# One weight cast of the recurrence tied behind the last turned block, gate differences in three steps, and first value products ahead of second transposes

## The chip, the core and the metric

The kernel runs on one NeuronCore of one Trainium2 chip. The core has a matrix engine (TensorE, written PE; its weight loads are written PEld), a vector engine (VectorE, DVE), an activation engine (ScalarE, ACT), a general engine (GpSimd, POOL) and a queue that issues most transfers (SyncE, SP). Each engine works through its own queue of instructions in the order in which the program was built; a wait on another engine's work stands in that queue too, and what is queued behind a waiting instruction waits with it. The metric is device time in microseconds, the median of several runs.

## The reference, cut to what matters

A hybrid block on 1024 tokens of width 1024, in float32: stick-breaking attention (8 heads of 64) and a gated linear recurrence (HGRN2, 4 heads of 128) on the same normalised input, merged by gates, then a squared-ReLU MLP and a final norm.

```
xn = rmsnorm(x, norm1_g)
u = xn @ w_in            # q, k, v | f, i, q, g of the recurrence | two gates
o_sb = stick_breaking_attention(q_sb, k_sb, v_sb)       # masked, cumulative in log space
k_hg = (1 - lb) * sigmoid(-f_raw)
o_hg = hgrn2_chunkwise(silu(q_hg), k_hg, i_hg, log_f)   # state carried over chunks
o_hg = rmsnorm(o_hg, hg_norm_g) * silu(g_hg)
merged = sigmoid(gate_sb + b) * (o_sb @ w_o_sb) + sigmoid(gate_hg + b) * (o_hg @ w_o_hg)
h = x + merged @ w_out
h = h + square(relu(rmsnorm(h, norm2_g) @ w_ff1)) @ w_ff2
return rmsnorm(h, final_g)
```

## The kernel before, in words

Every float32 operand of a product is split into a high part (cast to fp32r on ACT, `hi_copy`, line 156) and a low part (the difference, on DVE, `lo_sub`, line 161), and a product is three matrix products: high by high, high by low, low by high (`three`). So each weight matrix is loaded by SP, cast on ACT, subtracted on DVE, and then used by PE.

Work goes out in two lanes. The main lane is attention, then the recurrence. The fill lane, a `Stream` of jobs, is a list of projections (query and key of a head, the recurrence's f, q and i, the gates) whose bodies yield after a few products; `st.advance(n, upto)` lets n such steps out between two steps of the main lane. When a job starts, `prefetch` splits the weights of the next job and loads those of the one after. A builder then orders each engine's instructions from these two lanes and from the dependencies; `after(a, b)` adds the plain rule that a is not ordered ahead of b on its engine, with no semaphore.

Three places of this order matter here.

- The start. Tokens are normalised two blocks of 128 at a time (x0 and x1, then x2 and x3). `norm_transpose` turns a pair of blocks on PE into eight PSUM tiles xnt (one of 128 columns by 256 tokens for each of the eight parts of the width); ACT writes the high part xnh from each, DVE the low part xnl, and then the PSUM bank is free again. The fill job of this stage has the products for query and key of head 0 (pjqk, 24 of them for a pair of blocks) and for the values (pjv; with the high part wvh of the weight first, then with the low part wvl).
- The gate units (`RawUnit`, names wga0 to wga9; wga8 and wga9 belong to the output gates of the recurrence and stand inside the attention stage). Besides the split of its first half such a unit needs a difference of two weight pieces (`sub`, 128x1024), then a difference of the two halves of that (`sub`, 128x512), and the split of the result (names wga8t, wga9t: a cast on ACT and a subtraction on DVE). `Stream.step` calls `split_t` for the unit of the next job at the sixth step of the job in front of it, with all three at once.
- The end of attention. Each block of attention is turned on PE (pw), split into wTh on ACT and wTl on DVE (`turn`), and used by the value products po. The weight of the recurrence's input, `u_i`, has four pieces wir0 to wir3, which share two load buffers with other weights; its first piece is cast (wih0) when `hg_levels(0)` begins, with no rule on where that cast stands among the casts of the last turned blocks. In the recurrence's first step DVE and ACT make the pairs sd, which PE sums (sd products with ones).

Of the kernel before, what the change touches and what calls it, by code (L numbers as in the profile page):

```python
# [39 lines left out]
def kernel(  # L40
# [34 lines left out]
    def slot(name, dt=F32):  # L75
        return spool.tile([P, 1024], dt, tag="s", name=name)
# [28 lines left out]
    def after(ins, earlier):  # L105
        if earlier is not None and earlier.ins is not ins.ins:
            tc.add_manual_dep(ins.ins, earlier.ins.name, NOSYNC, reason="issue order")
        return ins
# [55 lines left out]
    def hi_lo(h, l, src):  # L164
        hi_copy(h, src)
        return lo_sub(l, src, h)
# [266 lines left out]
    class Unit:  # L433
# [5 lines left out]
        def split_t(self):  # L439
            pass  # L440
# [46 lines left out]
    class Stream:  # L487
# [36 lines left out]
        def step(self):  # L524

            if self.gen is None:
                if self.pos >= len(self.jobs):
                    return False
                self.steps = 0
                self._start()  # L530
            self.steps += 1
            if self.owed_t and self.steps == 6:
                self.owed_t.split_t(hg_level[0] or turn_lo[0])
                self.owed_t = None
            open_block("fill")
            if next(self.gen, StopIteration) is StopIteration:
                self.gen = None
                self.pos += 1
            return True
# [476 lines left out]
    def hg_levels(h):  # L1016
# [59 lines left out]
        for _, cs in halves():  # L1076
            after(mul(q[:, cs], q[:, cs], dec[:, cs]), pairs[3])
        if h == 0:
            u_i.split(1)
        yield  # L1080
        for l in range(7):
            H = 1 << l
# [159 lines left out]
    def sub(out, a, b):  # L1242
        return nc.vector.tensor_tensor(out=out, in0=a, in1=b, op=ALU.subtract)
# [40 lines left out]
    class RawUnit(Unit):  # L1284


        late = True

        def __init__(self, cb):
            dmas = [  # L1290
# [15 lines left out]
            hi_lo(h, l, ra)  # L1306
            self.hl = [(h, l)]

        def split_t(self, behind=None):
            if len(self.hl) == 1:  # L1310
                ra, rb = self.raw
                after(sub(rb, ra, rb), behind)
                sub(rb[:, 512:], rb[:, 512:], rb[:, 0:512])
                t = slot(f"{self.name}t", F32R)
                self.hl.append((t[:, 0:512], t[:, 512:]))
                hi_lo(*self.hl[1], self.raw[1][:, 512:])

    raw_units = [RawUnit(cb) for cb in range(NG)]

# [957 lines left out]
    st.advance(4, 1)  # L2277
    u_v.split(2)
    norm1((2, 3))
    st.advance(3, 1)  # L2280
    norm_transpose(xn, 0, 2, 2)
    u_v.split()
    st.advance(5, 1)
    norm1(range(4, NT))
    st.advance(8, 1)
    norm_transpose(xn, 1, 0, 4)
# [168 lines left out]
```

## Time and profile before

| what | us |
|---|---|
| median of 3 runs | 1439.45 (1439.32 to 1440.04) |
| the profiled execution's own time | 1439.79 |
| its span | 1437.8 |
| PE busy | 1424.4 (99%) |
| DVE busy | 1118.8 (78%) |
| ACT busy | 678.3 (47%) |

The span is the time between the first and the last instruction that the profile shows; the rest of the execution's time lies around it. Ends of matrix products are modelled and overlap the next product's start, so the time of a product in a sequence is read from start to start. A busy share says little about where the few microseconds lie that this change is about; they are read from the waits and from the rows in order of time. Buffer numbers are left out in the profile, so that wih in a row can be any of the four pieces.

### The profile page before, as it was taken

The page shows a single profiled execution, that of the slowest core. Times are in us where ns is not written, and L with a number is a line of the kernel's source. Part 1 is how long each engine was busy: PE and PEld are TensorE (multiplying, and loading weights), DVE is VectorE, ACT ScalarE, POOL GpSimd, SP SyncE. Part 2 cuts the span into 40 slices and gives each one's busy share as a digit, 9 for nine tenths or more (in the row PEclk, how much of TensorE's full clock was granted, in tenths as well). Part 3 has the DMA queues.
Part 4 walks back from the last instruction along what each step waited for, and adds up shares of the span by engine and source line. Part 5 has one row for each costly group of instructions (what it writes and reads, how often), then busy time and mean ns, then how long its engine had stood idle before and what let it go on. Part 6 is the DMA issues. An engine that isn't in the chain of part 4 may idle for free.

```text
span 1437.8 us, 19221 instructions
## 1 busy us (share of the span) xinstructions
PE 1424.4 (99%) x7056; PEld 1194.5 (83%) x7056; DVE 1118.8 (78%) x1537; ACT 678.3 (47%) x1177; POOL 148.0 (10%) x338
## 2 busy tenths in 40 slices
PE   9999999999999999999999999999999999999998
PEld 8888888888888888888888888888888888888886
DVE  6579999989678898798787898666666758668765
ACT  6356676663233345333244674444444433524343
POOL 3011223210011031000000300000000000000042
PEclk9999999999999999999999999999999999999999
DMA  7124435534015775545477405344446974776835
GB/s 238 27 62 115 110 85 92 89 60 133 22 45 154 232 184 196 167 158 180 153 275 249 176 31 197 131 143 145 161 153 212 349 264 164 259 275 253 274 103 182
DMA packets 161334, 233.54 MB, mean 162 GB/s; under 512 B 26028, under 2 KB 93144, under 8 KB 161240
## 3 DMA queue, kind: packets, MB, share of 16 engines
q1 hardware_dynamic: 145400, 190.11, 39.4%
q0 software_dynamic: 11520, 34.61, 9.4%
q10 hardware_dynamic: 4320, 7.60, 1.4%
q8 instruction: 55, 0.90, 0.3%
q14 instruction: 39, 0.32, 0.1%
HBM read 167.27 MB, written 65.01 MB: 162 GB/s over the span
## 4 chain that ended last, share of the span: by engine, by line
PE 92%; DVE 4%; ACT 1%; DMA 1%; issue 1%; POOL 0%; SPq 0%; DVEq 0%; ACTq 0%; POOLq 0%
PE pm L128 21%; PE pX L128 9%; PE pW L128 6%; PE pY L128 6%; PE pjqk L128 5%; PE gX L128 4%; PE gY L128 4%; PE pga L128 3%; PE pys L128 3%; PE pji L128 3%; PE pyh L128 3%; PE pjq L128 3%; PE pjv L128 3%; PE sl L128 3%; PE pwX L128 2%; PE po L128 2%
## 5 line engine op out<-in xcount | busy, mean ns | idle before, releaser
L156 ACT CAST whid<-w 128x1024 fp32r<-128x1024 f32 x30 | 31.6, 1054 | 154.6 <-PE pm L128 90.0
L808 DVE TENSOR_TENSOR_SCAN rm<-rm,bits 128x511 f32<-128x511 f32 (+7 forms) x72 | 87.1, 1218 | 9.6 <-ACT rm L786 9.4
L128 PE MATMUL pm<-wlod,sh 128*128 128x512 f32 x240 | 93.5, 390 | 0.0
L128 PE MATMUL pm<-whid,sl 128*128 128x512 f32 x240 | 93.4, 389 | 0.0
L128 PE MATMUL pm<-whid,sh 128*128 128x512 f32 x240 | 93.4, 389 | 0.0
L128 PE MATMUL pm<-tl,sh 128*128 128x512 f32 (+1 forms) x210 | 81.3, 387 | 0.0
L128 PE MATMUL pm<-th,sl 128*128 128x512 f32 (+1 forms) x210 | 81.3, 387 | 0.0
L128 PE MATMUL pm<-th,sh 128*128 128x512 f32 (+1 forms) x210 | 81.3, 387 | 0.0
L161 DVE TENSOR_TENSOR wlod<-w,whid 128x1024 fp32r<-128x1024 f32 x30 | 36.7, 1222 | 55.0 <-ACT whid L156 55.0
L161 DVE TENSOR_TENSOR sl<-sa,sh 128x1024 fp32r<-128x1024 f32 x56 | 68.2, 1218 | 0.0
L156 ACT CAST wTh<-pw 128x512 fp32r<-128x512 f32 (+2 forms) x96 | 43.9, 487 | 40.8 <-PE pw L131 39.6
L2091 POOL TENSOR_SCALAR fss<-fss 128x1 f32<-128x1 f32 x8 | 4.5, 560 | 562.1 <-ACT fsc L2086 561.6
L156 ACT CAST sh<-sa 128x1024 fp32r<-128x1024 f32 x56 | 57.2, 1046 | 6.1 <-DMA sa<-ad 6.1
L161 DVE TENSOR_TENSOR wTl<-pw,wTh 128x512 fp32r<-128x512 f32 (+2 forms) x96 | 50.5, 547 | 4.9 <-ACT wTh L156 4.6
L128 PEld LDWEIGHTS pm<-wlod,sh 128*128 128x128 f32 x240 | 45.1, 188 | 10.0 <-DVE wlod L161 0.4
L128 PEld LDWEIGHTS pm<-whid,sh 128*128 128x128 f32 x240 | 45.0, 187 | 9.4
L128 PEld LDWEIGHTS pm<-whid,sl 128*128 128x128 f32 x240 | 45.1, 188 | 9.1
L169 DVE TENSOR_TENSOR bt<-bt,rm 128x511 f32<-128x511 f32 (+7 forms) x72 | 49.0, 684 | 4.2 <-DVE rm L808 0.5
L128 PE MATMUL pX<-sql,t1h 128*128 128x512 f32 x128 | 50.0, 391 | 0.1
L128 PE MATMUL pX<-sqh,t1h 128*128 128x512 f32 x128 | 49.8, 389 | 0.0
L128 PE MATMUL pX<-sqh,t1l 128*128 128x512 f32 x128 | 49.8, 389 | 0.0
L786 ACT ACTIVATE rm<-z 128x511 f32<-128x511 f32 (+4 forms) x96 | 48.0, 500 | 3.5 <-DVE wTl L161 1.0
(933 smaller groups left out, 4475.5 us busy)
## 6 DMA issues: line engine op xcount, KB each, us to landing
w<-in_w_ff_dram SPq DMA_DIRECT2D x72, 512.0 KB, 6.2
sa<-ad SPq DMA_DIRECT2D x56, 512.0 KB, 7.0
ad<-a SPq DMA_DIRECT2D x32, 256.0 KB, 2.1
ad<-s SPq DMA_DIRECT2D x16, 512.0 KB, 5.5
tw<-in_w_out_dram POOLq DMA_DIRECT2D x24, 256.0 KB, 4.0
pr<-pd SPq DMA_DIRECT2D x10, 512.0 KB, 5.1
x<-in_x_dram SPq DMA_DIRECT2D x8, 512.0 KB, 9.9
xnl<-xnh POOLq DMA_DIRECT2D x8, 512.0 KB, 8.9
```

The costliest lines, as they stand in the source:

```text
L128: return pe(nc.tensor.matmul(*a, **k))
L156: hi_last[0] = after(in_turn("act", nc.scalar.copy(dst, src)), hi_behind[0])
L161: nc.vector.tensor_tensor(out=dst, in0=src, in1=hi.bitcast(F32), op=ALU.subtract),
L169: return nc.vector.tensor_tensor(out=out, in0=a, in1=b, op=ALU.mult)
L786: nc.scalar.activation(rm[:, s0 + c0 - 1 : s0 + m - 1], z[:, c0:m], AF.Sigmoid, scale=-0.125)
L808: sc = nc.vector.tensor_tensor_scan(out=rr, data0=rr, data1=bits[:, 1024 - nk + a : 1024 - nk + b][:, ::-1], initial=rm[:, b : b + 1] if i ...
L2091: nc.gpsimd.tensor_scalar(out=ssq, in0=ssq, scalar1=1.0 / D, scalar2=EPS, op0=ALU.mult, op1=ALU.add)
```

## The change

Three edits. In `Stream.step`, `split_t` of the next gate unit is called at steps 4, 6 and 8 and does one of its three parts each time, and the third part has the same rule on its place (behind the last turned block, or behind the last level of the recurrence) as the first. In `hg_levels`, the cast of the first piece of `u_i` gets the rule that it stands behind the cast of the last turned block (`turn_hi`). At the start, four steps of the fill job go out before the second pair of blocks is turned, where it was three, and four after it, where it was five.

```diff
--- before.py
+++ after.py
@@ -529,9 +529,10 @@
                 self.steps = 0
                 self._start()
             self.steps += 1
-            if self.owed_t and self.steps == 6:
-                self.owed_t.split_t(hg_level[0] or turn_lo[0])
-                self.owed_t = None
+            if self.owed_t and self.steps in (4, 6, 8):
+                self.owed_t.split_t(hg_level[0] or turn_lo[0], self.steps // 2 - 1)
+                if self.steps == 8:
+                    self.owed_t = None
             open_block("fill")
             if next(self.gen, StopIteration) is StopIteration:
                 self.gen = None
@@ -1076,7 +1077,9 @@
         for _, cs in halves():
             after(mul(q[:, cs], q[:, cs], dec[:, cs]), pairs[3])
         if h == 0:
+            hi_behind[0] = turn_hi[0]
             u_i.split(1)
+            hi_behind[0] = None
         yield
         for l in range(7):
             H = 1 << l
@@ -1285,6 +1288,7 @@
 
 
         late = True
+        turned = 0
 
         def __init__(self, cb):
             dmas = [
@@ -1306,14 +1310,18 @@
             hi_lo(h, l, ra)
             self.hl = [(h, l)]
 
-        def split_t(self, behind=None):
-            if len(self.hl) == 1:
-                ra, rb = self.raw
-                after(sub(rb, ra, rb), behind)
-                sub(rb[:, 512:], rb[:, 512:], rb[:, 0:512])
-                t = slot(f"{self.name}t", F32R)
-                self.hl.append((t[:, 0:512], t[:, 512:]))
-                hi_lo(*self.hl[1], self.raw[1][:, 512:])
+        def split_t(self, behind=None, upto=3):
+            ra, rb = self.raw
+            while self.turned < upto:
+                self.turned += 1
+                if self.turned == 1:
+                    after(sub(rb, ra, rb), behind)
+                elif self.turned == 2:
+                    after(sub(rb[:, 512:], rb[:, 512:], rb[:, 0:512]), behind)
+                else:
+                    t = slot(f"{self.name}t", F32R)
+                    self.hl.append((t[:, 0:512], t[:, 512:]))
+                    after(hi_lo(*self.hl[1], rb[:, 512:]), behind)
 
     raw_units = [RawUnit(cb) for cb in range(NG)]
 
@@ -2277,10 +2285,10 @@
     st.advance(4, 1)
     u_v.split(2)
     norm1((2, 3))
-    st.advance(3, 1)
+    st.advance(4, 1)
     norm_transpose(xn, 0, 2, 2)
     u_v.split()
-    st.advance(5, 1)
+    st.advance(4, 1)
     norm1(range(4, NT))
     st.advance(8, 1)
     norm_transpose(xn, 1, 0, 4)
```

How it moves instructions is shown at three places. The first is PE at the start, before: pjv are value products, wvl0 and wvl1 the low parts of the first two value weights, xnt00 to xnt07 the eight tiles of the second pair of blocks, x2 and x3 these blocks.

```order
L128 MATMUL pjv_0_312<-wvl0_291,xnh00_229 128x512 x2
L128 MATMUL pjv_1_317<-wvl0_291,xnh00_229 128x512 x2
L131 MATMUL xnt00_2_334<-ident_75,x2_165 128x128
L131 MATMUL xnt00_2_334<-ident_75,x3_169 128x128
L131 MATMUL xnt01_2_339<-ident_75,x2_165 128x128
...
L131 MATMUL xnt06_2_364<-ident_75,x3_169 128x128
L128 MATMUL pjv_0_312<-wvl1_295,xnh01_237 128x512
L131 MATMUL xnt07_2_369<-ident_75,x2_165 128x128
L131 MATMUL xnt07_2_369<-ident_75,x3_169 128x128
L128 MATMUL pjv_0_312<-wvl1_295,xnh01_237 128x512
L128 MATMUL pjv_1_317<-wvl1_295,xnh01_237 128x512 x2
L128 MATMUL pjqk0_0_265<-xnh00_229,wqk0whi_161 128x256
```

And in the changed kernel:

```order
L128 MATMUL pjv_0_312<-wvl0_291,xnh00_229 128x512 x2
L128 MATMUL pjv_1_317<-wvl0_291,xnh00_229 128x512 x2
L128 MATMUL pjv_0_312<-wvl1_295,xnh01_237 128x512 x2
L128 MATMUL pjv_1_317<-wvl1_295,xnh01_237 128x512 x2
L131 MATMUL xnt00_2_338<-ident_75,x2_165 128x128
L131 MATMUL xnt00_2_338<-ident_75,x3_169 128x128
...
L131 MATMUL xnt06_2_368<-ident_75,x3_169 128x128
L128 MATMUL pjqk0_0_265<-xnh00_229,wqk0whi_161 128x256
L128 MATMUL pjqk0_0_265<-xnl00_230,wqk0whi_161 128x256
L131 MATMUL xnt07_2_373<-ident_75,x2_165 128x128
L131 MATMUL xnt07_2_373<-ident_75,x3_169 128x128
L128 MATMUL pjqk0_0_265<-xnh00_229,wqk0wlo_162 128x256
```

All eight low value products stand ahead of the transposes now, and the last pair of transposes stands behind the first two products of pjqk.

The second place is DVE in the second and third head of attention, before: wga8r are the two pieces of gate unit 8, rm and bt the scan and the product of a block of attention, wTl0_2 the turned blocks that the next value products read.

```order
L887 TENSOR_TENSOR osb0_1031<-po0_0_1072,ot0_0_1077 64x256
L808 TENSOR_SCALAR rm0_3_1083<-rm0_3_1083,bits_98 128x511
L169 TENSOR_TENSOR bt0_3_1082<-bt0_3_1082,rm0_3_1083 128x511
L161 TENSOR_TENSOR KS2_1099<-pjqk2_0_996,KS2_1099 64x512
L161 TENSOR_TENSOR wTl0_1_0_1114<-pw0_2_0_1117,wTh0_1_0_1113 128x3x128
L1243 TENSOR_TENSOR wga8r1_844<-wga8r0_842,wga8r1_844 128x1024
L808 TENSOR_SCALAR rm1_7_1126<-rm1_7_1126,bits_98 128x511
L1243 TENSOR_TENSOR wga8r1_844<-wga8r1_844 128x512
L169 TENSOR_TENSOR bt1_7_1125<-bt1_7_1125,rm1_7_1126 128x511
L161 TENSOR_TENSOR wga8t_1140<-wga8r1_844,wga8t_1140 128x512
L161 TENSOR_TENSOR wTl0_2_0_1057<-pw0_4_0_1157,wTh0_2_0_1056 128x4x128
L161 TENSOR_TENSOR wTl0_2_4_1059<-pw0_4_1_1164,wTh0_2_4_1058 128x128
```

And in the changed kernel:

```order
L1246 TENSOR_TENSOR wga8r1_844<-wga8r0_842,wga8r1_844 128x1024
L809 TENSOR_SCALAR rm0_3_1083<-rm0_3_1083,bits_98 128x511
L161 TENSOR_TENSOR KS2_1100<-pjqk2_0_996,KS2_1100 64x512
L161 TENSOR_TENSOR wTl0_1_0_1115<-pw0_2_0_1118,wTh0_1_0_1114 128x3x128
L169 TENSOR_TENSOR bt0_3_1082<-bt0_3_1082,rm0_3_1083 128x511
L1246 TENSOR_TENSOR wga8r1_844<-wga8r1_844 128x512
L809 TENSOR_SCALAR rm1_7_1127<-rm1_7_1127,bits_98 128x511
L169 TENSOR_TENSOR bt1_7_1126<-bt1_7_1126,rm1_7_1127 128x511
L161 TENSOR_TENSOR wTl0_2_0_1057<-pw0_4_0_1154,wTh0_2_0_1056 128x4x128
L161 TENSOR_TENSOR wTl0_2_4_1059<-pw0_4_1_1161,wTh0_2_4_1058 128x128
L809 TENSOR_SCALAR rm1_7_1127<-rm1_7_1127,bits_98 128x512
L161 TENSOR_TENSOR wga8t_1178<-wga8r1_844,wga8t_1178 128x512
```

The two differences stand some rows earlier, and the last subtraction, wga8t, stands behind the turned blocks wTl0_2 and not ahead of them. On ACT the rows of this place keep their order. Gate unit 9 is moved in the same way in the last head, where its cast wga9t goes behind two block casts on ACT; gate unit 0 keeps its place.

The third place is ACT at the end of attention, before: wTh7 are casts of turned blocks of the last head, k2 and pp2 belong to the recurrence, p1_9 is a copy for gate 9, wq2h the cast of the next query weight.

```order
L786 ACTIVATE rm7_3_3653<-z7_3_0_3654 128x511
L789 ACTIVATE bt7_3_3652<-z7_3_0_3654 128x511
L156 COPY wih0_3824<-wir0_3726 128x1024
L156 COPY wTh7_1_0_3673<-pw7_2_0_3677 128x3x128
L910 ACTIVATE k2_3603<-pjf2_1_3608 128x512
L911 ACTIVATE pp2_3602<-pjf2_1_3608 128x512
L156 COPY wTh7_2_0_3626<-pw7_4_0_3702 128x4x128
L156 COPY wTh7_2_4_3628<-pw7_4_1_3709 128x128
L1345 COPY p1_9_3689<-pga9_3692 128x512
L156 COPY wq2h0_3722<-wq2r0_3486 128x1024
L1346 DMA pd9_112<-p1_9_3689 128x512
L156 COPY wTh7_1_0_3673<-pw7_3_0_3740 128x4x128
```

And in the changed kernel:

```order
L787 ACTIVATE rm7_3_3650<-z7_3_0_3651 128x511
L790 ACTIVATE bt7_3_3649<-z7_3_0_3651 128x511
L911 ACTIVATE k2_3604<-pjf2_1_3609 128x512
L156 COPY wTh7_1_0_3673<-pw7_2_0_3677 128x3x128
L912 ACTIVATE pp2_3603<-pjf2_1_3609 128x512
L156 COPY wTh7_2_0_3623<-pw7_4_0_3702 128x4x128
L156 COPY wTh7_2_4_3625<-pw7_4_1_3709 128x128
L1353 COPY p1_9_3689<-pga9_3692 128x512
L156 COPY wq2h0_3722<-wq2r0_3486 128x1024
L1354 DMA pd9_112<-p1_9_3689 128x512
L156 COPY wTh7_1_0_3673<-pw7_3_0_3740 128x4x128
L156 COPY wih0_3824<-wir0_3726 128x1024
```

The cast wih0 stands behind the last cast of a turned block, wTh7_1, and behind wq2h. On DVE its low part moves behind wq2l likewise. On SP the loads keep their order, but the buffers change hands: wir1 took the buffer of wir0 before and takes that of wq2 now.

## The prediction, made before the changed kernel was run

> **What bounds the kernel now.** I read the page's first part, then the list of waits of TensorE (PE), then the stages of the span, and last the rows in order of time at the places that the diff touches. The columns of a wait are total us, times, longest us.
>
> ```profile
> span 1437.8 us, 19221 instructions
> PE 1424.4 (99%) x7056; PEld 1194.5 (83%) x7056; DVE 1118.8 (78%) x1537; ACT 678.3 (47%) x1177; POOL 148.0 (10%) x338
> ```
> ```profile
> PE po L128 <- DVE wTl L161: 2.0, 6, 0.5
> PE po L128 <- ACT wTh L156: 1.4, 2, 0.9
> ```
> ```profile
> 343.00:530.00 187.00, 187.00 (x1107) 159.13 (x1107) 148.58 (x238) 64.82 (x162) 23.40 (x28) 1.00 0.41 121
> 530.00:834.00 304.00, 304.00 (x1463) 254.04 (x1461) 251.18 (x345) 132.09 (x197) 31.43 (x56) 1.00 0.57 192
> ```
>
> PE is the bound. Between 343 and 834 us it never stops (187.00 of 187.00, 304.00 of 304.00, granted clock 1.00). So the change can only win back PE idle time, and what it wins before 343 us stays won if the engines behind PE come forward with it. The value products po, which wait for turned blocks, are the only waiters of weight (2.0 + 1.4 us). The change touches three places: about 17, 107 and 322 us.
>
> **Third place, the recurrence's first weight cast (322 us).** A row of time is: start, length, engine, line, operation, out<-in, [idle before it <- who ended that].
>
> ```profile
> 320.43 1.05 ACT L156 CAST wih<-wir 128x1024 fp32r<-128x1024 f32 x1 [4.84 <-DMA wir<-in_w_in_dram]
> 321.38 0.47 ACT L156 CAST wTh<-pw 128x384 fp32r<-128x384 f32 x1
> 323.35 0.63 ACT L1345 COPY p<-pga 128x512 f32<-128x512 f32 x1
> 323.82 1.10 ACT L156 CAST wq2h<-wq2r 128x1024 fp32r<-128x1024 f32 x1
> 329.21 1.05 ACT L156 CAST wih<-wir 128x1024 fp32r<-128x1024 f32 x1 [3.13 <-DMA wir<-in_w_in_dram]
> ```
> ```profile
> 320.27 0.40 PE L128 MATMUL pga<-xnh,wga9wlo 128*128 128x512 f32 x1
> 321.88 0.60 PE L131 MATMUL pw<-ident,bt 128*128 128x128 f32 x4
> 323.37 0.38 PE L128 MATMUL po<-wTh,V 128*128 128x256 f32 x1 [0.89 <-ACT wTh L156]
> 324.10 0.39 PE L128 MATMUL po<-wTl,V 128*128 128x256 f32 x1 [0.34 <-DVE wTl L161]
> 325.52 0.40 PE L128 MATMUL pgq<-xnh,wga9t 128*128 128x512 f32 x1
> ```
>
> ScalarE (ACT) sits idle for 4.84 us at the cast of wir0, which has not landed, and the casts wTh of turned blocks stand behind it in its queue. PE pays: the twelve po products start at 323.37 and their second at 324.10. Without the wait the first would follow the four transposes of 321.88 at 322.34 (0.116 each, from the nine in 1.20 us quoted for the first place), the second 0.12 later at 322.46, and from the second to pgq it is 1.42 us as now (324.10 to 325.52): pgq at 323.88 and not at 325.52, so 1.64 us. If the transposes issue closer, as their modelled ends allow, it is some 0.1 more: 1.64 to 1.76. In the new order the cast stands behind the last block's cast, so this wait hides no block. Who is queued behind the tied cast now? The copy ot of the po just computed, and the second weight cast; PE needs neither before the recurrence's first sums.
>
> That makes the second weight piece, wir1, what is late next. Its rows:
>
> ```profile
> 313.96 0.68 DVE L161 TENSOR_TENSOR wga9t<-wga9r,wga9t 128x512 fp32r<-128x512 f32 x1
> 324.16 1.21 DVE L161 TENSOR_TENSOR wil<-wir,wih 128x1024 fp32r<-128x1024 f32 x1
> 325.29 1.22 DVE L161 TENSOR_TENSOR wq2l<-wq2r,wq2h 128x1024 fp32r<-128x1024 f32 x1
> 330.30 1.23 DVE L161 TENSOR_TENSOR wil<-wir,wih 128x1024 fp32r<-128x1024 f32 x1 [2.01 <-ACT wih L156]
> 336.05 0.68 DVE L161 TENSOR_TENSOR sd_l<-sd_x,sd_h 128x512 fp32r<-128x512 f32 x1
> 336.79 0.50 PE L128 MATMUL sd<-sd_l,ones 128*128 128x512 f32 x1
> ```
> ```profile
> 314.67 5.69 DMA wir<-in_w_in_dram
> ```
> ```profile
> 325.43 0.37 SPq L136 DMA_DIRECT2D wir<-in_w_in_dram  x1
> ```
>
> wir1 is issued at 325.43, when the piece before it is split (324.16 + 1.21), and is cast at 329.21: 3.78 us. From that cast a chain without slack runs on VectorE (DVE): wil at 330.30, sd_l ending at 336.73, the sd product at 336.79. After the change PE reaches that product 1.7 us earlier, so the chain must come forward as much or PE waits there. It does, by my sum: p is copied when the pga product of 320.27 is out (+0.42, as elsewhere on ACT), 320.69; wq2h follows 0.47 later, 321.16, and ends at 322.26; wq2l runs on DVE from 322.30 to 323.52. In the changed order wir1 takes the buffer that wq2l frees, so it is issued at 323.56, 1.87 us earlier, and with 3.78 us everything to the sd product moves by 1.87. So PE can keep the whole of its 1.64 to 1.76; I take 1.7.
>
> The gate's third step (wga9t, 313.96) is now issued behind two block subtractions and one output sum, some 2.1 us later by the DVE rows between, and frees wir0's buffer that much later. With its 5.69 us wir0 lands at about 322.5, just before its cast can start (323.1). Cover: the tie itself. The loads on SP keep their order, and no queue of POOL is passed.
>
> **Second place, gate differences in three steps (107 us).**
>
> ```profile
> 105.83 0.62 ACT L156 CAST wga8t<-wga8r 128x512 fp32r<-128x512 f32 x1 [3.02 <-DVE wga8r L1243]
> ```
> ```profile
> 107.83 0.39 PE L128 MATMUL po<-wTl,V 128*128 128x256 f32 x1 [0.46 <-DVE wTl L161]
> 123.03 0.39 PE L128 MATMUL po<-wTl,V 128*128 128x256 f32 x1 [0.23 <-DVE wTl L161]
> ```
> ```profile
> 95.40:123.00 27.60, 26.46 (x148) 22.30 (x146) 26.54 (x38) 19.53 (x43) 6.58 (x24) 1.00 0.46 117
> ```
> ```profile
> 106.49 0.69 DVE L161 TENSOR_TENSOR wga8t<-wga8r,wga8t 128x512 fp32r<-128x512 f32 x1
> 107.09 0.88 DVE L161 TENSOR_TENSOR wTl<-pw,wTh 128x512 fp32r<-128x512 f32 x2
> 118.37 0.42 DVE L169 TENSOR_TENSOR bt<-bt,rm 128x255 f32<-128x255 f32 x1 [0.48 <-DVE rm L808]
> 122.31 1.13 DVE L161 TENSOR_TENSOR wTl<-pw,wTh 128x512 fp32r<-128x512 f32 x2
> ```
>
> ACT waits 3.02 us for the second difference, again with block casts behind it, and the last gate subtraction (0.60 to the next start) stands ahead of wTl on DVE. In the new order the subtraction is behind wTl, so po starts 0.6 to 0.75 us earlier than 107.83. But the row of this stretch has DVE busy for 26.54 of 27.60 us (third figure; the first is PE), and between 107 and 122 its only idle row is 0.48 at 118.37: the same instructions in another order end at the same time. PE then meets wTl at 122.31 that much too early and waits there instead of at 107.83. What remains is the drain between a scan and the product that reads it, which other instructions now fill: 0.08 to 0.28 us by my count of the pairs. Bounds: 0 and 0.75; I take 0.25, near the lower, since the row at 122.31 decides. The unit of gate 0 keeps its order, so it costs nothing.
>
> **First place, value products ahead of the second transposes (17 us).**
>
> ```profile
> 16.76 1.07 PE L128 MATMUL pjv<-wvl,xnh 128*128 128x512 f32 x4
> 17.67 0.27 PE L131 MATMUL xnt<-ident,x 128*128 128x128 f32 x1
> 18.14 1.20 PE L131 MATMUL xnt<-ident,x 128*128 128x128 f32 x9 [0.20 <-DVE x L646]
> 18.50 3.03 ACT L336 ACTIVATE xnh<-xnt,prm 128x256 fp32r<-128x256 f32 x8 [2.73 <-PE xnt L131]
> 19.01 3.22 DVE L339 SCALAR_TENSOR_TENSOR xnl<-xnt,prm,xnh 128x256 fp32r<-128x256 f32 x8 [0.93 <-ACT xnh L336]
> 22.50 2.36 DVE L161 TENSOR_TENSOR wvl<-wvr,wvh 128x1024 fp32r<-128x1024 f32 x2 [0.27 <-ACT wvh L156]
> ```
> ```profile
> 21.53 2.86 PE pjqk L128 x24
> ```
>
> Four value products (0.91 us: 16.76 to 17.67) move ahead, into the wait for x3 (0.34 us) and beyond, so the transposes start at 18.58, and ACT and DVE, which free their banks, 0.56 us later. The last three transposed pairs each wait for a bank; at DVE's 0.39 per tile they run at 20.1, 20.5 and 20.9, with two of the 24 pjqk products between, and the other 22 (0.119 each) end near 23.85, where they now end at 24.23 (24.39 less the 0.16 by which the chain's times lag the starts). That is 0.35 to 0.4 won. The next value products need wvl, which comes 0.56 later too: 22.50 + 0.56 + 1.2 = 24.26, against 24.3 for the first product that reads it. No slack, so the bounds are 0.4 won and 0.15 lost; I take 0.35 won, since no wait is worked out.
>
> **Sum.** 0.35 + 0.25 + 1.7 = 2.3 us off the profiled execution's own 1439.79 us (span 1437.8 and 2.0 around it): 1437.5. That execution was 0.34 above the median of the runs, 1439.45, so I forecast 1439.45 - 2.3, or 1437.2.
>
> **Rivals.** The gain of the second place is kept. It needs DVE 0.7 us earlier at 122.31: the 0.25 of drains and the idle 0.48 at 118.37, for which the profile shows no cause, gone. Against it: that idle time ends no wait on PE. Then 0.35 + 0.73 + 1.76 = 2.84 and 1436.6. Chance 0.20.
>
> wir1 lands late. If it takes 5.69 like wir0, it is cast at 329.25 as now, the recurrence does not come forward, and PE waits the 1.7 us at the sd product instead: 0.6 is left, 1438.9. For it: wir0's own row. Against: wir1's own row, with the same neighbours. Chance 0.13.
>
> The slower side: the same landing, once it takes over 5.69 + 0.6 = 6.3 us, makes the kernel slower. The slowest load near by:
>
> ```profile
> wq2r<-in_w_in_dram SPq DMA_DIRECT2D x1, 512.0 KB, 7.1
> ```
>
> With 7.1 us the sd product is 1.4 later than now and the time 1440.3. Chance 0.12, with whatever wait I have not seen. The Trainium skill, "DMA: Bandwidth & Descriptors", section "Anatomy of one DMA", fits one transfer issued from GpSimd as 2.0 us plus its bytes at 436 GB/s; that would be an estimate of 3.2 us for these 512 KB, by which the two landing rivals would hardly have a chance. The rows above (3.78, 5.69, 7.1, issued from SP) do not agree with it, and the chances go by the rows.
>
> That the change does not do what it says is excluded by the order for the cast and the products; for the third gate unit it is so, and costs nothing.
>
> **How the numbers follow.** The forecast has 0.55, with 1436.6 to 1438.0 as its own range (1.49 us off, with 0.15 lost at the first place and 1.64 won at the third, to 2.84). The other 0.45 are the rivals above. The range 1435.9 to 1439.3 takes in the first two rivals and leaves out the slower one. A measurement of this kernel can tell about 0.2%, 2.9 us, from no change. Faster than that: the half of the first rival, and what the three terms may be undersized by, 0.24. Slower than that needs a landing of over 9 us or an unseen wait, 0.10. The rest, 0.66, is within it.
>
> **What would show it.** In the changed profile the 4.84 us idle ahead of wih on ACT and PE's waits at 323.37 and 324.10 should be gone, wir1 be issued near 323.0 (325.43 less 1.87 and the 0.6 of the places before), and the sd product wait no more than 0.1 us. At the second place the po near 107 should start about 0.7 earlier, and the one near 122.4 should wait about 0.5 longer. At the first, pjqk should end about 0.35 earlier. The prediction is wrong if PE waits over 0.5 us at sd, or if DVE turns out to have idle time between 107 and 122 that another order removes.

## The result and the profile after

| | before | changed |
|---|---|---|
| median of 19 runs each, same chip | 1439.60 us | 1436.88 us |
| range of those runs | 1439.02 to 1440.38 | 1436.68 to 1438.67 |
| ratio to before | | 0.9982, 95% interval 0.9975 to 0.9989 |
| span of the profiled execution | 1437.8 | 1434.9 |
| own time of the profiled execution | 1439.79 | 1436.76 |

The change wins 2.7 us where 2.3 were forecast. It is 0.18%, just under the 0.2% that the prediction gave as what a measurement tells from no change, though the interval leaves no change out.

Where the 2.9 us of the two spans lie is read by matching every matmul of one trace with the same matmul of the other and taking, for each short stretch of time, the median by which PE is ahead (PE's lead). PE of the changed kernel is 0.45 us ahead at 25 us, 0.24 from 40 to 100, 0.81 from 123 to 320, 2.62 at 325, 2.77 at 340 and 2.92 from 350 to the end. So the first place left 0.24, the second 0.57 and the third 2.1.

Third place: ACT's timeline of the changed kernel (start, duration, instruction; in brackets the idle time ahead and what ended it; dots stand for rows left out).

```profile
320.35 1.05 ACT L156 CAST wq2h<-wq2r 128x1024 fp32r<-128x1024 f32 x1
321.67 0.59 ACT L156 CAST wTh<-pw 128x512 fp32r<-128x512 f32 x1 [0.28 <-PE pw L131]
322.16 1.05 ACT L156 CAST wih<-wir 128x1024 fp32r<-128x1024 f32 x1
...
326.42 1.05 ACT L156 CAST wih<-wir 128x1024 fp32r<-128x1024 f32 x1 [2.83 <-DMA wir<-in_w_in_dram]
```

The cast of wih stands behind the last wTh, and the 4.84 us of idle time ahead of it are gone. PE's timeline of the same kernel:

```profile
321.39 0.36 PE L128 MATMUL po<-wTh,V 128*128 128x256 f32 x1
321.59 0.28 PE L128 MATMUL po<-wTl,V 128*128 128x256 f32 x1
...
333.20 0.39 PE L128 MATMUL pjq<-xnh,wq2l 128*128 128x512 f32 x1
333.43 0.39 PE L128 MATMUL sd<-sd_h,ones 128*128 128x512 f32 x1
```

Neither po (323.37 and 324.10 before) nor sd waits. The loads, by SP's timeline and the view of the transfers (the last figure is the time from issue to landing; of the four wir loads the profile tells the landing of the first alone):

```profile
316.25 0.37 SPq L136 DMA_DIRECT2D wir<-in_w_in_dram  x1
...
322.69 0.37 SPq L136 DMA_DIRECT2D wir<-in_w_in_dram  x1
```

```profile
wir<-in_w_in_dram SPq DMA_DIRECT2D x4, 512.0 KB, 3.6
wq2r<-in_w_in_dram SPq DMA_DIRECT2D x1, 512.0 KB, 5.0
```

wir1 was issued at 322.69 (forecast 323.0), and ACT took it up 3.73 us later (forecast 3.78). wir0 took 3.6 us where the prediction reckoned with 5.69.

Second place, on ACT, PE and DVE:

```profile
104.28 0.62 ACT L156 CAST wga8t<-wga8r 128x512 fp32r<-128x512 f32 x1 [1.71 <-DVE wga8r L1246]
```
```profile
106.83 0.39 PE L128 MATMUL po<-wTl,V 128*128 128x256 f32 x1 [0.44 <-DVE wTl L161]
...
122.22 0.38 PE L128 MATMUL po<-wTl,V 128*128 128x256 f32 x1 [0.31 <-DVE wTl L161]
```
```profile
106.09 0.88 DVE L161 TENSOR_TENSOR wTl<-pw,wTh 128x512 fp32r<-128x512 f32 x2
...
117.38 0.42 DVE L169 TENSOR_TENSOR bt<-bt,rm 128x255 f32<-128x255 f32 x1
...
121.50 1.13 DVE L161 TENSOR_TENSOR wTl<-pw,wTh 128x512 fp32r<-128x512 f32 x2
```

po starts 1.0 us earlier than at 107.83. At 122 it waits for DVE again, by 0.08 us more than before (0.31 against 0.23), not by the forecast 0.5. For DVE itself came forward: wTl is at 121.50 instead of 122.31. And the product that had 0.48 us of idle time ahead now has no bracket; it starts 0.10 us after the scan ends.

First place, PE, ACT and DVE, with the chain's row for pjqk:

```profile
16.74 1.98 PE L128 MATMUL pjv<-wvl,xnh 128*128 128x512 f32 x8
18.55 1.25 PE L131 MATMUL xnt<-ident,x 128*128 128x128 f32 x10
20.02 0.83 PE L131 MATMUL xnt<-ident,x 128*128 128x128 f32 x4 [0.21 <-DVE xnl L339]
```
```profile
21.31 2.64 PE pjqk L128 x22
```
```profile
18.97 3.03 ACT L336 ACTIVATE xnh<-xnt,prm 128x256 fp32r<-128x256 f32 x8 [3.20 <-PE xnt L131]
```
```profile
37.52 5.36 DVE L339 SCALAR_TENSOR_TENSOR xnl<-xnt,prm,xnh 128x512 fp32r<-128x512 f32 x8 [0.17 <-ACT xnh L336]
```

pjqk ends at 23.95 by the chain, where it ended at 24.39: 0.44 won, a little over the forecast 0.35. But ACT's xnh starts at 18.97 instead of 18.50, and this 0.47 us of lateness on ACT and DVE is still 0.31 at the next group of transposes, as the same row of the kernel before shows:

```profile
37.21 5.36 DVE L339 SCALAR_TENSOR_TENSOR xnl<-xnt,prm,xnh 128x512 fp32r<-128x512 f32 x8 [0.17 <-ACT xnh L336]
```

### The profile page after: what moved, and what is told of

Its sections match the earlier page's. It is cut to its first block, busy times and chain, and to the rows that moved or that the text cites. A ratio compares the mean times of both kernels' runs of the same rounds, so it can differ in the third digit from the quotient of the medians.

```text
span 1434.9 us, 19220 instructions
## 1 busy us (share of the span) xinstructions
PE 1422.9 (99%) x7056; PEld 1193.9 (83%) x7056; DVE 1118.7 (78%) x1537; ACT 678.1 (47%) x1177; POOL 148.3 (10%) x338
## 4 chain that ended last, share of the span: by engine, by line
PE 95%; DVE 3%; ACT 1%; issue 0%; DMA 0%; POOL 0%; SPq 0%; DVEq 0%; ACTq 0%
PE pm L128 21%; PE pX L128 9%; PE pW L128 6%; PE pY L128 6%; PE pjqk L128 5%; PE gX L128 4%; PE gY L128 4%; PE pga L128 4%; PE pys L128 3%; PE pji L128 3%; PE pjv L128 3%; PE pyh L128 3%; PE pjq L128 3%; PE po L128 3%; PE sl L128 3%; PE pwX L128 2%
```

## The experiments

Every kernel was timed against the kernel before on the same chip. The ratios' intervals are about 0.1% wide on each side, 1.3 us, so a difference of some tenths is read from the traces, and from the times only where they are far enough apart. Profiled executions of this kernel differ by up to 0.35 us at its start, before any edit acts. So a gain at a place is taken as the change of PE's lead across that place. Lines that do not matter are left out of the code shown.

### Each place alone

The tie alone:

```diff
         if h == 0:
+            hi_behind[0] = turn_hi[0]
             u_i.split(1)
+            hi_behind[0] = None
```

> The kernel before with the third place alone: the recurrence's first weight cast is ordered behind the last turned block's cast, nothing else is changed. Theory A (the prediction's sum): PE's two waits of 1.74 us at 322 to 324 us go and nothing after them changes, 1.7 us won. Theory B (from the two traces): PE comes 1.78 us forward at those two waits, another 0.1 at the sd product and 0.15 near 349 us, because the recurrence's weights are also ready earlier there; 2.0 to 2.1 us won. Theory C: the gain needs the new third step of gate 9, which in the changed kernel let the first recurrence load land in 3.64 us after 5.69 us before; then this kernel wins under 1 us and the trace shows ACT or PE waiting for that load again.

Measured: 1437.61 us against 1439.47, ratio 0.9987 (0.9978 to 0.9996), 1.86 us won. In the trace PE gains 1.78 us at the two po, 0.14 more by 340 and 0.12 by 350. Theory C is out: the gain does not need gate 9's new third step. The three gains, 2.04 us in all, are theory B's. ACT has wih behind wTh, as in the changed kernel:

```profile
322.45 0.59 ACT L156 CAST wTh<-pw 128x512 fp32r<-128x512 f32 x1 [0.22 <-PE pw L131]
322.93 1.05 ACT L156 CAST wih<-wir 128x1024 fp32r<-128x1024 f32 x1
```

The time, 1.86 us, lies between theories A (1.7) and B (2.0 to 2.1) and tells neither apart, for its interval is 0.6 to 3.2 us. One reason why the trace shows more is in the next kernels.

The value products alone:

```diff
-    st.advance(3, 1)
+    st.advance(4, 1)
     norm_transpose(xn, 0, 2, 2)
     u_v.split()
-    st.advance(5, 1)
+    st.advance(4, 1)
```

> The kernel before with the first place alone: all four steps of first value products ahead of the second transposes. Theory A (the prediction's sum): 0.35 us won, and kept to the end. Theory B (from the two traces): 0.45 won at the end of pjqk, 0.11 of it given back at the wait for wvl, and another 0.11 to 0.14 at the next transposes near 38 us, since ACT and DVE run 0.47 us later from 18.5 us on; 0.2 to 0.25 us is left. The trace tells them apart by PE's position after 40 us; the times alone can't.

Measured: 1439.33 us against 1439.47, ratio 1.0 (0.9991 to 1.0008). The trace has 0.40 us at 25 us, 0.29 at 35 and 0.16 from 40 us on: theory B. It gains 0.3 more at 322 us, where nothing was edited. There its wir0 landed 5.41 us after its issue, not 5.69. The same shows in the next kernel (5.42) and in the first (5.49), while the kernel before with one instruction more on DVE, further below, had 5.76. So this load differs by up to 0.35 us between executions with the same order, and every lead that is read across this place is uncertain by as much. Against the three quicker loads, the 1.74 us of waits of the profiled execution before are 0.2 to 0.3 us long.

Gate 8 in three steps, gate 9 and the others in one (shown is the part in `Stream.step`, against the kernel before; `split_t` in three parts is that of the changed kernel, with the rules on its place arranged so that a call for all three parts does what it did before):

```diff
-            if self.owed_t and self.steps == 6:
-                self.owed_t.split_t(hg_level[0] or turn_lo[0])
-                self.owed_t = None
+            if self.owed_t and self.steps in (4, 6, 8):
+                if self.owed_t is raw_units[KT]:
+                    self.owed_t.split_t(hg_level[0] or turn_lo[0], self.steps // 2 - 1)
+                elif self.steps == 6:
+                    self.owed_t.split_t(hg_level[0] or turn_lo[0])
+                if self.steps == 8:
+                    self.owed_t = None
```

> The kernel before with the second place alone, for gate 8 (the differences near 100 to 110 us in three steps; gate 9 keeps its single step). Theory A (the prediction's sum): DVE sets the end, so what po wins at 107 us is lost again at 122 us but for 0.25 us. Theory B (from the two traces): DVE itself comes forward by 0.55 to 0.6 us, of which about 0.35 are gaps between a scan and the product behind it and 0.2 to 0.25 the idle 0.48 us ahead of the product at 118.37, which shrinks to 0.1; PE wins 0.6 us and keeps it.

Measured: 1438.99 us against 1439.47, ratio 0.9996 (0.9987 to 1.0005). In the trace PE gains 0.75 us at 107 and has 0.57 of it left behind 123: theory B, the same figure as in the changed kernel. (The time alone could not tell it from no change.) The idle time ahead of the small product is 0.10.

Gate 9 and the others in three steps, gate 8 in one, no tie (the same lines with `is not`):

> The kernel before with the differences of gate 9 alone in three steps (gate 8 in one step, and the recurrence's first weight cast not tied). The third step is some 2.4 us later in the program and frees the recurrence's first load that much later, and that cast still stands ahead of the turned block's on ACT. Theory A (a load of 512 KB takes here what it took before, 5.69 us): the cast starts some 2.4 us later than at 320.43, and the kernel is about 2.4 us slower. Theory B (from the two traces: the load takes 3.64 us, since the load of wq2 is issued 2.5 us earlier and has landed): the cast starts near 320.7 us, and the kernel is 0.2 to 0.5 us slower. Theory C (PE's waits there are not set by this load): no change.

Measured: 1439.16 us against 1439.47, ratio 0.9997 (0.9988 to 1.0006); not slower, and all three theories missed. In the trace PE gains 0.73 us at 322 us, of which 0.3 can be the slow load of the execution that it is read against. The load is indeed issued 2.7 us later (317.35 instead of 314.67), but lands after 3.61 us, at 320.96. The cast also has less behind it, for the order on ACT is another one:

```profile
317.80 0.47 ACT L156 CAST wTh<-pw 128x384 fp32r<-128x384 f32 x1
...
321.32 1.05 ACT L156 CAST wih<-wir 128x1024 fp32r<-128x1024 f32 x1 [2.54 <-DMA wir<-in_w_in_dram]
322.27 0.75 ACT L156 CAST wTh<-pw 128x512 fp32r<-128x512 f32 x2
```
```profile
322.90 0.39 PE L128 MATMUL po<-wTh,V 128*128 128x256 f32 x1 [0.17 <-ACT wTh L156]
323.63 0.39 PE L128 MATMUL po<-wTl,V 128*128 128x256 f32 x1 [0.34 <-DVE wTl L161]
```

The first block cast and the two activations (k, pp), which were queued behind wih before, now go ahead of it. That is the reading of the trace; no kernel tests the order alone. With the tie this gain has nothing left to act on: the tie alone wins 2.04 us in the trace at this place, the whole change 2.1.

### The first place with two products

```diff
                     for tb in range(2):
                         for kt in (k0, k0 + 1):
                             v_part(tb, kt, hi, not hi)
+                        if not hi and k0 and not tb:
+                            yield
                     yield
...
     st.advance(4, 1)
     norm_transpose(xn, 0, 2, 2)
     u_v.split()
-    st.advance(4, 1)
+    st.advance(5, 1)
```

> The changed kernel with two of the four value products ahead of the second transposes, the other two after them. Theory A (the prediction: the first place wins its 0.35 us and keeps it): no gain over the changed kernel, within 0.1 us. Theory B (the traces: the four products start the transposes, and with them ACT's and DVE's work, 0.47 us later, and 0.11 and 0.1 us are given back for it at the wait for wvl and near 38 us): two products (0.45 us) just fill PE's wait for x3, the transposes start near 18.1 as before, ACT's xnh stays at 18.50, pjqk still ends 0.45 us earlier, and PE is 0.4 to 0.45 us ahead of the kernel before at 42 us instead of 0.2: 0.2 us faster than the changed kernel.

Measured: 1436.64 us against 1439.56, ratio 0.9979 (0.997 to 0.9988). Its trace has PE 0.2 us ahead of the changed kernel from 40 us on, to the end: theory B.

```profile
16.72 1.53 PE L128 MATMUL pjv<-wvl,xnh 128*128 128x512 f32 x6
18.08 1.25 PE L131 MATMUL xnt<-ident,x 128*128 128x128 f32 x10
```
```profile
18.50 3.03 ACT L336 ACTIVATE xnh<-xnt,prm 128x256 fp32r<-128x256 f32 x8 [2.73 <-PE xnt L131]
```
```profile
37.05 5.36 DVE L339 SCALAR_TENSOR_TENSOR xnl<-xnt,prm,xnh 128x512 fp32r<-128x512 f32 x8 [0.17 <-ACT xnh L336]
```

Two products fill exactly the wait for x3. The transposes start at 18.08 with no gap, ACT is where it was before (18.50), and DVE's row at 37 us is 0.16 earlier than in the kernel before, not 0.31 later.

### Gate 8's differences out of the busy stretch

```diff
             if len(nxt) > 1:
                 nxt[1].load()
+                if nxt[1] is raw_units[KT]:
+                    nxt[1].split_t(None, 2)
```

> The changed kernel with gate 8's first two differences (1.21 and 0.68 us on DVE) made as soon as their weights are loaded, near 58 us, where DVE waits for ACT; the third step stays near 108 us. Theory A (DVE sets the end of every po from 95 to 123 us; its time there falls by 1.14 and 0.6 us): PE's waits at 106.8 (0.68) and 121.6 us (0.55) go, 1.0 to 1.2 us won over the changed kernel, up to what another wait gives back. Theory B (ACT and the scores set the pace there, DVE only follows): po at 107 starts no earlier, and the kernel is the same within 0.3 us. Theory C: the differences near 58 us delay the first scan (59.6 us) by 0.5 to 1 us and PE waits for it later; slower.

Measured: 1435.61 us against 1439.56, ratio 0.997 (0.9958 to 0.9981). This is the changed kernel, with its four value products, and this edit alone; it is 1.0 us under the kernel with two products, on the same chip. PE's lead over the changed kernel grows by 1.1 us between 100 and 125 us: theory A.

```profile
58.78 1.23 DVE L1248 TENSOR_TENSOR wga8r<-wga8r,wga8r 128x1024 f32<-128x1024 f32 x1 [1.50 <-DMA wga8r<-in_w_in_dram]
60.04 0.69 DVE L1248 TENSOR_TENSOR wga8r<-wga8r 128x512 f32<-128x512 f32 x1
...
116.60 0.43 DVE L169 TENSOR_TENSOR bt<-bt,rm 128x255 f32<-128x255 f32 x1 [0.48 <-DVE rm L811]
```

The two differences push the first scan 0.9 us back, and nothing feels it. PE's wait near 107 is gone, and that near 121 is down from 0.55 us of lost time to 0.25. But the idle 0.48 us is back, with gate 8's third step still where the change put it. So that idle time does not come of the three steps as such.

Both edits together:

> The changed kernel with both of the edits above: two value products ahead instead of four, and gate 8's first two differences near 58 us. If the two work at places that do not touch each other, the gains add: 1.2 to 1.4 us faster than the changed kernel, about 1435.5 us. If PE's earlier start of 0.2 us is met by a later wait on DVE, only the second counts.

Measured: 1435.48 us, ratio 0.997 (0.9959 to 0.9981). In the trace PE's lead over the changed kernel grows by 1.3 us up to 125 us, so the two add there; in the medians only 0.13 of the second 0.2 shows, which is within their scatter.

### The idle 0.48 us

Counting every record of DVE in the trace from 0, its waits on semaphores too, the small product is record 191 in each of the six kernels so far that have the idle time (before, the tie alone, the value products alone, gate 9 alone, the early differences, and these with two products), and record 190 in each of the four that don't (changed, gate 8 alone, two products, and the kernel with wir1 loaded twice that stands below). The three steps need one wait less ahead of it. The test is one more instruction far ahead of it:

```diff
         mul(lb, le[:, 0:4], lmx)
+        mul(lb, le[:, 0:4], lmx)
```

> The kernel before with one DVE instruction of 0.16 us more near 46 us (the lower bounds' last product is written a second time), where DVE has over 1 us of slack. It moves everything behind it by one place in DVE's list. What is asked: whether the idle 0.48 us ahead of the product at 118.37 belongs to a place in the list. That product is DVE's record 191 (counting every record from 0, waits too) wherever the idle time shows; where it is record 190 the idle time is 0.10. Theory A (a stop of about 0.45 us stands ahead of DVE's record 191, whatever that is): record 191 is now the wait ahead of the product, the stop lies under the scan of 0.67 us, the idle time falls to 0.1 us, and PE wins 0.25 to 0.4 us at 123 us. Theory B (the idle time comes of what the neighbours do): 0.48 stays and nothing is won.

> The changed kernel with the same one DVE instruction more near 46 us. Theory A (a stop ahead of DVE's record 191): record 191 is the product near 117.4 again, its idle time of 0.10 becomes 0.48, DVE is 0.3 to 0.4 us later at the block subtraction of 121.50, and PE loses that much there: what the second place wins falls from 0.57 to about 0.25, the prediction's term. The idle 0.51 us ahead of the product at 189.74 (record 319 in the changed kernel) falls to 0.13, which PE does not feel. Theory B (neighbours): no difference but the 0.16 us that are hidden.

> The kernel with two value products ahead and gate 8's first two differences near 58 us, and the same one DVE instruction more near 46 us. Without it the product near 116.4 is DVE's record 191 and has 0.48 us idle ahead. Theory A (a stop ahead of DVE's record 191): the idle time falls to 0.1, PE's remaining wait of 0.25 us at 120.7 goes, and the kernel is about 0.25 us faster than without the instruction, near 1435.2 us. Theory B (neighbours): the same as without it.

DVE's timelines of the three, in this order:

```profile
118.31 0.42 DVE L169 TENSOR_TENSOR bt<-bt,rm 128x255 f32<-128x255 f32 x1
```
```profile
117.65 0.42 DVE L169 TENSOR_TENSOR bt<-bt,rm 128x255 f32<-128x255 f32 x1 [0.48 <-ACT bt L791]
```
```profile
116.18 0.42 DVE L169 TENSOR_TENSOR bt<-bt,rm 128x255 f32<-128x255 f32 x1
```

Theory A in all three: it goes from the kernel before, comes into the changed one, and goes from the best. PE gains 0.40 us at 123 in the first (1438.89 us against 1439.18, ratio 0.9998, 0.9989 to 1.0007), loses 0.20 in the second (1436.85, ratio 0.9984, 0.9976 to 0.9993), and gains 0.27 in the third, against the kernel with both edits (1435.37, ratio 0.9974, 0.9964 to 0.9985). The sizes are in the range forecast but for the second, which lost 0.2 instead of 0.3 to 0.4.

The other half of the second expectation holds too. In the changed kernel a product at 189.74 is record 319, 128 behind 191, with 0.51 us idle ahead; in the kernel before it is record 320:

```profile
189.74 0.82 DVE L169 TENSOR_TENSOR bt<-bt,rm 128x639 f32<-128x639 f32 x1 [0.51 <-DVE rm L809]
```
```profile
190.18 0.82 DVE L169 TENSOR_TENSOR bt<-bt,rm 128x639 f32<-128x639 f32 x1
```

With one instruction more in the changed kernel, the wait is record 319, and the product follows its scan by 0.13 us again. PE does not feel this one.

The times of the first two kernels do not tell them from the kernels without the instruction; the trace does. The last kernel has the lowest median of all, though the 0.1 us to the kernel with both edits are within their scatter. Its eight runs (1435.08 to 1436.06) lie wholly under the eleven of the changed kernel with the same extra instruction, on the same chip (1436.58 to 1438.08).

### What a late wir1 costs

```diff
-                for lo_c, n, src in dmas:
+                for lo_c, n, src in dmas * (2 if self.name == "wi" and i == 1 else 1):
```

> The changed kernel with the second load of the recurrence's weights made twice into the same buffer, one after the other (the same data; a probe of what its landing is worth). Issued near 322.7 us it lands some 3.6 us later than in the changed kernel, 7.3 us after its issue. Theory A (the prediction's slower rival: there is hardly slack between this load and the sd product): the cast that waits for it starts near 330.0 instead of 326.4, PE waits 3.0 to 3.6 us at sd, and the kernel is about that much slower than the changed one, and 0.4 to 1 us slower than the kernel before. Theory B (the chain from this load to sd has over 1 us of slack, since sd waits for ACT's and DVE's other work): under 2.5 us slower than the changed kernel, and not slower than before.

Measured: 1440.93 us against 1439.56, ratio 1.0007 (0.9998 to 1.0016). ACT takes the load up 8.80 us after its issue at 322.92, 5.3 us later than in the changed kernel, and PE loses 3.0 us at sd. SP issued the second load at 326.52, 3.6 us behind the first and not right after it, and the third piece's load at 327.00 instead of 324.49, so the edit delays more than the one landing. The eleven runs spread from 1439.06 to 1441.40 us, and the profiled one, at 1439.98, is 0.95 under their median, so the trace shows a milder case.

```profile
331.72 1.05 ACT L156 CAST wih<-wir 128x1024 fp32r<-128x1024 f32 x1 [3.67 <-DMA wir<-in_w_in_dram]
```
```profile
335.52 0.50 PE L128 MATMUL sd<-sd_l,ones 128*128 128x512 f32 x1 [1.17 <-DVE sd_l L161]
336.83 0.50 PE L128 MATMUL sd<-sd_h,ones 128*128 128x512 f32 x1 [0.81 <-ACT sd_h L156]
```

The loss at sd is theory A's, but the delay was 5.3 us and not 3.6, and the time is 1.4 us above the kernel before where theory A had 0.4 to 1, so neither theory is borne out. A smaller delay, with a quarter of the load made again:

```diff
                     load(dst[:, :, lo_c : lo_c + n], src)
+                    if self.name == "wi" and i == 1:
+                        load(dst[:, :, lo_c : lo_c + n // 4], src[:, :, : n // 4])
```

> The changed kernel with a quarter of the recurrence's second load (128 KB) made again behind it, into the same buffer with the same data: a smaller delay of its landing than the whole load made twice, which moved the cast behind it from 326.42 to 331.72 us (5.30) and cost 3.2 us in the trace, 2.1 less than the delay. The delay here should be 1.5 to 3 us. Theory A (the prediction: hardly any slack, so a landing 1.7 us late costs 1.7 less the 0.1 of slack): PE waits at the sd products the whole delay less 0.1 to 0.2 us, 1.4 us or more. Theory B (the chain from this load to sd has some 2 us of slack, as the whole load made twice would have it): PE waits under 0.5 us, or none, and the kernel is within 0.5 us of the changed one.

```profile
329.33 1.05 ACT L156 CAST wih<-wir 128x1024 fp32r<-128x1024 f32 x1 [1.41 <-DMA wir<-in_w_in_dram]
```
```profile
334.38 0.49 PE L128 MATMUL sd<-sd_l,ones 128*128 128x512 f32 x1 [0.30 <-DVE sd_l L161]
335.69 0.50 PE L128 MATMUL sd<-sd_h,ones 128*128 128x512 f32 x1 [0.82 <-ACT sd_h L156]
```

Measured: 1438.95 us against 1439.19, ratio 0.9999 (0.999 to 1.0008). The cast is 2.9 us later than in the changed kernel. PE loses 1.6 us at the sd products and 0.8 more by 365 us, 2.4 in all. The truth is between the theories, much nearer to A. In both kernels the order on ACT and DVE around this load changed with it (the sigmoid of the gate went ahead of the cast), so how much slack the changed kernel's own order has is not settled by them.

## Why the prediction was right or wrong

**The sum.** 2.3 us was forecast and 2.7 measured; the time, 1436.88, lies between the forecast 1437.2 and the first rival's 1436.6, and in the range. Faster by 0.18% is within the 0.2% that got the 0.66. That the sum is off by no more is in part luck: by the traces two of its terms are 0.3 and 0.4 too small, the third 0.1 too large, and the slow load of the execution that they are read against may make up 0.2 to 0.3 of what is missing.

**Third place: right, the term slightly small.** 1.7 was forecast. The two waits of PE went whole, with nothing late behind them, and that was 1.78 us in the trace. Some 0.25 us more came by 350 us. It had not been counted, and its cause stays open: that the recurrence's later weights are ready earlier would fit, but two kernels without the tie also gain at the same sd products (gate 9 alone 0.16 us, the kernel before with one DVE instruction more 0.15, and 0.09 more by 350). Against the gain stands that the profiled execution of the kernel before had a slow load at this place (5.69 us, where three other kernels with the same order had 5.41 to 5.49, and one 5.76), which can make the trace's gain 0.2 to 0.3 too large. The times of the tie alone, 1.86 us, fit that (2.04 in the trace, less 0.2 to 0.3), but do not prove it.

**The landing of wir0: a wrong step without a price.** The prediction had it issued some 2 us later and landing after its 5.69, just before the cast. It was issued later but landed after 3.64 us. The gate's earlier first step also let wq2's load go 2.5 us earlier, and the two no longer overlap. The prediction took one duration for a load whose company the change altered. That it is wq2's load and no other is not shown: two transfers tw on POOL's queue run beside both, and the last of them overlaps wir0 for 4.4 us before and 1.0 us after. With the tie the load had 2.3 us to spare ahead of the cast, so it cost nothing. In the kernel with gate 9 alone the same slip is seen at work: 2.4 us lost by theory A, 0.4 to 0.7 won in the trace.

**Second place: wrong, the step that failed.** It was the sentence that the same instructions in another order end at the same time, with 0.25 us for the drains as all that remains. DVE came forward by 0.57 us, and PE kept as much. The drains were a little more than reckoned: with the idle 0.48 us put back by one instruction, 0.37 is left. The other 0.2 is that idle time. The prediction saw it, found no cause in the profile, and let it stay: "that idle time ends no wait on PE". It does: it stands ahead of the wTl that ends PE's wait at 122, and one DVE instruction more in the kernel before took 0.40 us off PE there. What the prediction named as its failure, idle time on DVE between 107 and 122 that another order removes, is what happened. But the order removed it by its number of waits, not by its sequence.

**First place: the mechanism right, the term too large.** 0.35 was forecast, 0.16 to 0.24 left. The gain at pjqk was 0.44, and the lower bound's reason, wvl later by 0.47 us, took 0.10 of it. What the sum lacked is that the lateness of ACT and DVE does not end at wvl: it stands in the queue up to the next transposes, and takes another 0.1 there. The kernel with two products, which leaves ACT and DVE where they were, has that 0.2 us.

**The rivals.** The kept gain of the second place was the case that came true in most of its size (0.57 of 0.73 us), for the reason it named. wir1 did not land late: 3.73 us, as the row of wir1 itself said, not that of wir0. Its price was right to about 1 us: with a landing 6.5 us after the issue the kernel took 0.2 us less than the kernel before, where the prediction put the point from which it is slower at 6.3, and with 8.8 us it took 1.4 more, where that price gives 2.5. Both probes moved other work too, so this is no exact test.

## What to carry to other kernels

An idle time for which the profile shows no cause is not fixed: before it is left in a sum, look for the same gap in other kernels by the instruction's place in its engine's list, and move the place by one cheap instruction. On an engine that is busy through a stretch, work whose inputs are ready long before (here two subtractions, 1.9 us on DVE) belongs in an earlier stretch where that engine waits, rather than in smaller pieces in the same one. When work is pulled into a wait, take as much as the wait holds and no more, since whatever it delays on the other engines is paid for at their next meeting.

## What the hardware showed that was not expected

DVE stops for 0.40 to 0.43 us between a wait that is over and the instruction behind it, at record 191 and again at record 319 of its list. Where a wait or an instruction behind a long one stands there, the stop lies under the work that runs and costs 0.1 us or nothing. Both positions lie 128 apart, and the rest of the traces bears the step out. Each of the fourteen has some 200 idle times of DVE over 0.3 us. In nearly all of them the instruction behind starts within 0.25 us of the end of its wait. Where it starts later than that, and the profile tells when the wait ended, it is record 191, 319, 1599 or 1855, and 1599 and 1855 are 10 and 12 times 128 behind 319. The one exception is an instruction near 1105 us that starts 1.65 us behind its wait in every trace, at five different numbers. At 1599 stands a difference of weights, so the stop does not belong to the products of attention. In the changed kernel:

```profile
1028.48 0.69 DVE L1246 TENSOR_TENSOR w_12r<-w_12r,w_12r 128x512 f32<-128x512 f32 x1 [1.27 <-DMA w_12r<-in_w_ff_dram]
```

By the trace's times 0.45 of these 1.27 us lie behind the end of the wait. ACT has idle times of 0.32 us of this kind at its records 575, 703 and 1471 in some of the kernels, which lie on the same step, but longer ones at other numbers too. The page of the changed kernel has two queues that carry code, one with transfers of 16.4 KB (0.90 MB in 55 packets) and one with 8.2 KB (0.32 MB in 39):

```profile
q8 instruction: 55, 0.90, 0.3%
q14 instruction: 39, 0.32, 0.1%
```

In the changed kernel one of the 8.2 KB packets starts 0.75 us behind record 319 and one 0.9 us behind record 191. The Trainium skill, "Runtime: NRT & Kernel Launch", section "Instruction fetch mechanics", says that an engine's code comes in blocks of 16 KiB or 256 instructions, and that crossing into the next is mostly hidden. By that a stop every 256 instructions would be looked for; the traces have a queue with 8.2 KB packets and stops 128 records apart. That the stop is the change of block is argued from these numbers, not shown. At the other places 128 apart up to record 1215 no such stop shows in the changed kernel, and what exactly DVE waits for stays open.

A load of 512 KB on SP's queue, the recurrence's first piece, took 3.36 to 3.91 us in the nine kernels where the load ahead of it on this queue had landed, and 5.41 to 5.76 us in the five where it was issued 4.0 us behind one that was still under way; that one then took 6.8 to 7.2 us instead of 4.4 to 5.0. The transfers tw on POOL's queue stand differently beside them too, so how much of this is SP's queue is not separated. The 3.2 us that the prediction worked out from the Trainium skill's page "DMA: Bandwidth & Descriptors", section "Anatomy of one DMA", are near the first group; the two slower rows on which the prediction rested instead (5.69 and 7.1) were of loads that overlapped.
